# New durations in the planner of a two-block kernel, and a guard between two rotary tasks

## The chip, the cores and the metric

The kernel runs on one core of a Trainium2 chip. The metric is device microseconds for one launch; the kernel before was timed three times. Throughout, TensorE's columns of the trace are called PE (matmuls) and PEld (weight loads), VectorE is DVE, ScalarE is ACT, GpSimd is POOL, and SyncE, which issues all DMAs here, is SP.

## The reference

256 rows of width 2048, fp32, go through two blocks.

```python
x = x + attention(rms_norm(x, mixer_norm))            # 32 query heads, 4 key heads of 64, window 128
x = x + swiglu(rms_norm(x, ffn_norm))                 # 5632 wide
for l in range(2):                                    # second block
    mod = silu(c) @ ada_w[l] + ada_b[l]               # shift, scale, gate
    h = rmsnorm(x, g_pre[l]) * (1 + scale) + shift
    y = mlstm_mixer(h) if l == 0 else band_attention_mixer(h, k, v)
    x = x + gate * rmsnorm(y, g_post[l])
```

Queries and keys of the first block are normalised per head and rotated (rotary embedding, `apply_rope`). The mixer of l = 0 projects to 8 heads of q, k (256 wide) and v, o, z (512 wide), convolves q and k over time, forms a decay-weighted 256 x 256 product for each head, and multiplies the normalised result by sigmoid(o) * silu(z). For l = 1, keys and values come from a modulated copy of x, and 16 heads of 128 attend over a band with a bias.

## The kernel before, in words

**Weights.** Every weight matrix streams from memory once, in slots of 2 x 128 rows by 512 columns (`strm`, tile `w`). Each slot is split into a high part by ACT (`wh`, a cast to fp32r) and the rest by DVE (`wl`). With the activations split likewise (`xh`, `xl` or `ah`, `al`), one product is three fp32r matmuls. A k-tile of a chunk (128 rows, here called a step) is 12 matmuls of 256 columns or 6 of 512; a slot is two steps. There are 816 slots. These are the main matmuls (tile `mm`).

**Stages.** P1 is the attention block (`kv_task`, `att_task`, `att_half` beside the projections), P2 the FFN, P3 the mLSTM mixer (per head a chunk of q and k, then v, o, z; `conv_task`, `num_task`, `y_task`), P4 the band attention (`band_head`). From the start of P2 on, the modulation vectors are computed beside all this on DVE: 256 mv steps (`mv_run`), each with a load of 512 KB and two multiply-adds on `mvacc`; after 8 of them `mv_reduce` splits the sum (`acch` on ACT, `accl` on DVE) and lets PE sum over partitions with two pairs of matmuls (tile `bg`).

**The planner.** The program's order is fixed on the host while it is built. A `Clock` keeps one planned time for each engine. The wrapper `Eng` adds a planned duration for each instruction as it is emitted (lines 46 to 67); nothing of it runs on the chip. Everything beside the main matmuls is a Python generator in a queue `bgq`. After each step of main matmuls, `pump` asks `due` of each task:

```python
if task[2]:
    return task[1] + LAG <= clk.eng["pe"]
return (task[1] <= clk.eng["pe"] + task[4]
        and max(clk.eng["v"], clk.eng["s"]) <= clk.eng["pe"] + LOAD)
```

`task[1]` is the planned end of the task's last instruction, `LAG` is 0.3, `LEAD` (the usual `task[4]`) 1.0 and `LOAD` 6.0 planned us. The first branch is that of a part with matmuls: it goes into PE's order behind the first step that ends at least 0.3 planned us after its inputs. Each engine runs its own instructions in the order in which they were emitted, so a background matmul that stands too early makes PE wait. `stall` advances the tasks without main matmuls between, where the next chunk needs a result. The planner knows neither DMA times nor a wait for a buffer, nor table loads of ACT. A generator that yields `HOLD` is asked again at the next pump. `mv_step` starts an mv step when the planned time of the last one's next load, 5.0 planned us after it, is at most 0.3 ahead of PE's clock.

**norm_rope** (lines 589 to 609) takes a tile of heads through its mean of squares, the multiplication with the result, two POOL products into `rb`, a DVE product into `rc` and a DVE sum. `rb` and `rc` have one buffer each.

Of the kernel before, what the change touches and what calls it, by code (L numbers as in the profile page):

```python
# [11 lines left out]
F32R = mybir.dt.float32r  # L12
# [31 lines left out]


class Eng:
    RATE = {"v": 1.0 / 960, "s": 1.0 / 1400, "g": 1.0 / 480}
    BASE = {"v": 0.13, "s": 0.26, "g": 0.15}

    def __init__(self, eng, key, clock):  # L50
        self._e, self._k, self._c = eng, key, clock
# [1 line left out]
    def __getattr__(self, name):  # L53
        fn = getattr(self._e, name)

        def f(*a, **k):
            dst = k["out"] if "out" in k else a[0]
            n = int(np.prod(dst.shape[1:]))
            if self._k == "pe":
                m = k["rhs"] if "rhs" in k else a[2]  # L60
                fast = m.dtype == F32R
                dur = max(n, 256) / 2400 if fast else 4 * max(n, 64) / 2400
            else:
                dur = self.BASE[self._k] + n * self.RATE[self._k]
            self._c.spend(self._k, dur)
            return fn(*a, **k)  # L66
        return f
# [13 lines left out]
def kernel(ctx: ExitStack, tc: tile.TileContext, i: dict, out: bass.AP):  # L81
# [45 lines left out]
    sc = keep.tile([P, KD], F32, name="sc")  # L127
    ident = kc[:, K_ID:K_ID + P]

# [1 line left out]
    PF, SP = 4, 3  # L131
    order = []
    loaded = {}
# [29 lines left out]
    HOLD = 16  # L163
# [118 lines left out]
    plan = []  # L282
# [27 lines left out]
        for c in range(width, 4):  # L310
            add_chunk(chs[c])

# [1 line left out]
    mv = {"gen": None, "pace": 0.0, "acc": 0.0, "t": 0.0, "done": set(), "sent": set()}  # L314
    gt = {}

# [84 lines left out]
    busy = {"kv", "tab", "rst"}  # L401
# [21 lines left out]
        while lab not in mv["done"]:  # L423
            stall()

# [1 line left out]
    def rstd(dst, ss, n):  # L427
        shp = list(ss.shape)
        v = small.tile(shp, F32, tag="rv", bufs=2, name="rv")
        r = small.tile(shp, F32, tag="rr", bufs=2, name="rr")  # L430
        q = small.tile(shp, F32, tag="rq", bufs=2, name="rq")
        V.tensor_scalar(v, ss, 1.0 / n, EPS, op0=ALU.mult, op1=ALU.add)
        V.tensor_scalar(r.bitcast(I32), v.bitcast(I32), -0.5, 1597463007.0, op0=ALU.mult, op1=ALU.add)
        for it in range(3):
            V.tensor_mul(q, r, r)
            V.scalar_tensor_tensor(q, q, -0.5, v, op0=ALU.mult, op1=ALU.mult)
            V.scalar_tensor_tensor(dst if it == 2 else r, q, 1.5, r, op0=ALU.add, op1=ALU.mult)
# [82 lines left out]
        wrote("a", kt0, n, 2 if sl is None else 1)  # L520
        free(1)

# [1 line left out]
    p1 = ExitStack()  # L524
    q1 = p1.enter_context(tc.tile_pool(name="p1", bufs=1))
    make_identity(nc, ident)
# [62 lines left out]
    def norm_rope(src, H, w, t, dst):  # L589
        n = H * 64  # L590
        s3 = src.rearrange("p (h d) -> p h d", d=64)
        sq = q1.tile([P, CW], F32, tag="sq", bufs=1, name="sq")
        S.activation(sq[:, :n], src, ACTF.Square)
        ss = q1.tile([P, H], F32, tag="ss", bufs=2, name="ss")
        V.tensor_reduce(ss, sq[:, :n].rearrange("p (h d) -> p h d", d=64), AX.X, ALU.add)
        ri = q1.tile([P, H], F32, tag="ri", bufs=2, name="ri")
        rstd(ri, ss, 64)
        ri = ri.unsqueeze(2)
        yield
        V.tensor_mul(s3, s3, ri.to_broadcast([P, H, 64]))  # L600
        b = q1.tile([P, 8, 64], F32, tag="rb", bufs=1, name="rb")
        ta, tb = tab[:, w, t, 0], tab[:, w, t, 1]
        G.tensor_mul(b[:, :H, 0:32], s3[:, :, 32:64], tb[:, 0:32].unsqueeze(1).to_broadcast([P, H, 32]))
        G.tensor_mul(b[:, :H, 32:64], s3[:, :, 0:32], tb[:, 32:64].unsqueeze(1).to_broadcast([P, H, 32]))
        c = q1.tile([P, 8, 64], F32, tag="rc", bufs=1, name="rc")[:, :H]
        V.tensor_mul(c, s3, ta.unsqueeze(1).to_broadcast([P, H, 64]))
        yield
        V.tensor_add(dst, c, b[:, :H])
        yield

    def kv_task(kv):
        k3 = big[:, 0:1536].rearrange("p (a b c) -> p a b c", a=2, b=4)
        V.memset(k3, 0.0)
        while "tab" in busy:
            yield HOLD
        for t in range(2):
            yield from norm_rope(kv[:, t], 4, 1, t, k3[:, t, :, 64:128])
        for gg in range(2):
            yield 2
            bs = []  # L620
            for g in (2 * gg, 2 * gg + 1):
                b = bank([P, 2, T])
                for t in range(2):
                    PE.transpose(b[:, 0, t * P:(t + 1) * P], k3[:, t, g, 64:192], ident)
                    PE.transpose(b[:, 1, t * P:(t + 1) * P], k3[:, t, g, 0:128], ident)
                bs.append(b)
            yield
            for j in range(2):
                S.copy(kpad[:, 2 * gg + j], bs[j])
                free(1)  # L630
        busy.discard("kv")
# [5 lines left out]
    def att_task(g, qs):  # L637
        while "tab" in busy:
            yield HOLD
        for t in range(2):  # L640
            yield from norm_rope(qs[:, t], 8, 0, t, qs[:, t].rearrange("p (h d) -> p h d", d=64))
        qT = q1.tile([P, 2, 4, P], F32, tag="qT", bufs=2, name="qT")
        yield 2
        bs = []
        for t in range(2):
            b = bank([P, 4, P])
            for j in range(4):
                PE.transpose(b[:, j], qs[:, t, j * P:(j + 1) * P], ident)
            bs.append(b)
        yield  # L650
        for t in range(2):
            S.copy(qT[:, t], bs[t])
            free(1)
        add_bg(att_half(g, 0, qT))
        add_bg(att_half(g, 1, qT))
# [68 lines left out]
        yield  # L724
        hilo(4 * g, b, 4, slice(t * P, (t + 1) * P))

    # P1 plan
    def kv_done(ps):
        while "rst" in busy:
            stall()  # L730
        clk.cur = clk.eng["pe"]
        kv = q1.tile([P, 2, 256], F32, name="kv")
        for t in range(2):
            S.activation(kv[:, t], ps[t][:, 0:256], ACTF.Copy, scale=rst[:, t:t + 1])
            S.activation(vsb[:, t], ps[t][:, 256:512], ACTF.Copy, scale=rst[:, t:t + 1])
        add_bg(kv_task(kv))
# [47 lines left out]
    add_out([mk("tok", wload(i["w_o"], 0, n * CW), "a", KD, wo_done(n)) for n in range(4)], [4, 6], 3)  # L784
    will("x", 0, KD)

    # P2 plan
    pools = {}

    def enter2():  # L790
# [64 lines left out]
            chs[3].done, chs[3].part = None, down_part  # L855
        add_out(chs, [nk // SL - 2], 2)

    # P3 plan
    def ahead(gen, n):
        for _ in range(n):  # L860
            next(gen)
        add_bg(gen, 8.0)
# [224 lines left out]
                chs[3].done, chs[3].part = None, lambda ps, t: aout_half(ps, t, 3, 1)  # L1087
            add_out(chs, [6], 2)

    # P4 plan  # L1090
    qz = big[:, D:].rearrange("p (a k t) -> p a k t", a=2, t=T)
    def enter4():
        drain()
# [181 lines left out]
    chs[3].done, chs[3].part = None, fin_part  # L1275
    add_out(chs, [6], 2)

# [1 line left out]
    def start_stats():  # L1279
        for n in range(4):  # L1280
            yield
            for t in range(2):
                sumsq(q1, x[:, t, n * CW:(n + 1) * CW], ssx[:, t, n:n + 1])
        x_rstd()
        busy.discard("rst")
        yield
        S.activation(sc, cols[:, C_C:C_C + KD], ACTF.Silu)
# [88 lines left out]
```

## Time and profile before

| | us |
|---|---|
| runs, in order of time | 2548.68, 2553.22, 2559.36 |
| median | 2553.22 |
| the profiled execution, its span | 2553.0 (no other time of it is given) |
| PE busy in it | 2492.9 (98%) |
| DVE busy | 1783.5 (70%) |
| ACT busy | 1222.0 (48%) |
| POOL busy | 167.4 (7%) |
| mean DMA rate | 225 GB/s |
| mean granted TensorE clock | 0.990 |

Nearly all instructions have line 66 of the wrapper, so the trace is read by tiles and by stretches. PE is busy almost throughout; what matters is where it isn't, and what it waits for there. The page counts 34863 instructions.

### The profile page before, as it was taken

What the parts mean: (1) busy time and instruction counts of PE and PEld (TensorE: products, weight loads), DVE (VectorE), ACT (ScalarE), POOL (GpSimd) and SP (SyncE); (2) the same over time, 40 slices, a digit from 0 to 9 for tenths busy, and PEclk for the clock granted to TensorE, in tenths of its full rate; (3) what the DMA queues carried; (4) which work ended last, traced back from release to release, by engine and by line L of the source; (5) the groups of instructions that cost most, each with busy time, mean ns of one, the idle gap of its engine ahead of it and who ended that gap; (6) DMA issues with size and microseconds to landing.
All of it is one profiled execution on the core that took longest, in us unless ns stands there. A gap on an engine that the chain in (4) does not pass through costs nothing.

```text
span 2553.0 us, 34863 instructions
## 1 busy us (share of the span) xinstructions
PE 2492.9 (98%) x12816; PEld 2083.1 (82%) x12816; DVE 1783.5 (70%) x2788; ACT 1222.0 (48%) x1696; POOL 167.4 (7%) x174
## 2 busy tenths in 40 slices
PE   8999999999999999899999999999999989999998
PEld 6767888888888888778788778888888789899986
DVE  6885777777777777778778777765454564477755
ACT  5655544334443444555445444445444454455553
POOL 0231000000000000201101010001001120000000
PEclk9999999999999999999999999999999999999999
DMA  6434788888888887568878888856656546677854
GB/s 207 149 102 146 232 277 269 278 277 276 275 272 278 275 276 261 164 208 277 262 239 254 267 276 275 269 159 190 184 163 197 166 133 189 185 262 251 261 189 149
DMA packets 319083, 575.57 MB, mean 225 GB/s; under 512 B 21664, under 2 KB 56608, under 8 KB 318912
## 3 DMA queue, kind: packets, MB, share of 16 engines
q1 hardware_dynamic: 318912, 573.35, 69.7%
q8 instruction: 100, 1.64, 0.3%
q14 instruction: 71, 0.58, 0.1%
HBM read 571.18 MB, written 2.10 MB: 225 GB/s over the span
## 4 chain that ended last, share of the span: by engine, by line
PE 78%; issue 6%; DVE 6%; DMA 5%; ACT 3%; SPq 0%; POOL 0%; ACTq 0%; DVEq 0%; POOLq 0%
PE mm L66 73%; PE bg L66 5%; DMA w<-in_a_w_in_dram 4%; DVE wl L66 3%; ACT wh L66 2%; DVE mvacc L66 1%; DMA w<-in_b_w_in_dram 1%; DMA rb<-in_rel_dram 0%; DMA w<-in_a_w_out_dram 0%; DVE pr L66 0%; ACT sq L66 0%; DVE xl L66 0%; DMA x<-in_x_dram 0%; ACT big L66 0%; DVE big L66 0%
## 5 line engine op out<-in xcount | busy, mean ns | idle before, releaser
L66 DVE TENSOR_TENSOR wl<-w,wh 128x1024 fp32r<-128x1024 f32 x816 | 1010.3, 1243 | 627.9 <-ACT wh L66 616.9
L66 ACT CAST wh<-w 128x1024 fp32r<-128x1024 f32 x816 | 853.4, 1050 | 947.9 <-PE mm L66 747.6
L66 PE MATMUL mm<-wh,xh 128*128 128x512 f32 x1760 | 702.5, 399 | 0.0
L66 PE MATMUL mm<-wh,xl 128*128 128x512 f32 x1760 | 696.5, 396 | 4.1 <-DVE xl L66 4.1
L66 PE MATMUL mm<-wl,xh 128*128 128x512 f32 x1760 | 696.4, 396 | 1.7 <-DVE wl L66 1.7
L66 DVE SCALAR_TENSOR_TENSOR mvacc<-mvt,sc,mvacc 128x512 f32<-128x512 f32 x512 | 393.0, 768 | 11.6 <-DMA mvacc<-in_ada_b_dram 1.6
L66 PEld LDWEIGHTS mm<-wh,xl 128*128 128x128 f32 x1760 | 331.0, 188 | 85.2 <-DVE xl L66 5.0
L66 PEld LDWEIGHTS mm<-wl,xh 128*128 128x128 f32 x1760 | 331.3, 188 | 79.8 <-DVE wl L66 2.2
L66 PEld LDWEIGHTS mm<-wh,xh 128*128 128x128 f32 x1760 | 331.3, 188 | 79.1 <-issue 2.3
L66 PE MATMUL mm<-xh,wh 128*128 128x256 f32 x1280 | 367.8, 287 | 8.2 <-DVE xh L66 8.2
L66 PE MATMUL mm<-xl,wh 128*128 128x256 f32 x1280 | 364.5, 285 | 0.8 <-DVE xl L66 0.7
L66 PE MATMUL mm<-xh,wl 128*128 128x256 f32 x1280 | 362.8, 283 | 0.0
L66 PE MATMUL mm<-wh,al 128*128 128x512 f32 x864 | 341.9, 396 | 3.3 <-DVE al L66 3.3
L66 PE MATMUL mm<-wh,ah 128*128 128x512 f32 x864 | 345.0, 399 | 0.0
L66 PE MATMUL mm<-wl,ah 128*128 128x512 f32 x864 | 341.7, 395 | 0.1
L66 PEld LDWEIGHTS mm<-xh,wh 128*128 128x128 f32 x1280 | 246.6, 193 | 11.0 <-DVE xh L66 6.1
L66 PEld LDWEIGHTS mm<-xl,wh 128*128 128x128 f32 x1280 | 246.2, 192 | 3.5 <-DVE xl L66 3.0
L66 PEld LDWEIGHTS mm<-xh,wl 128*128 128x128 f32 x1280 | 245.9, 192 | 0.0
L66 PEld LDWEIGHTS mm<-wh,al 128*128 128x128 f32 x864 | 162.5, 188 | 43.0 <-DVE al L66 3.8
L66 PEld LDWEIGHTS mm<-wh,ah 128*128 128x128 f32 x864 | 162.4, 188 | 41.5 <-issue 4.0
L66 PEld LDWEIGHTS mm<-wl,ah 128*128 128x128 f32 x864 | 162.4, 188 | 38.5 <-issue 0.7
L66 POOL TENSOR_TENSOR so<-so,sz 128x512 f32<-128x512 f32 x16 | 30.4, 1897 | 713.5 <-ACT sz L66 370.3
(187 smaller groups left out, 1405.2 us busy)
## 6 DMA issues: line engine op xcount, KB each, us to landing
mvt<-in_ada_dram SPq DMA_DIRECT2D x192, 512.0 KB
w<-in_a_w_in_dram SPq DMA_DIRECT2D x192, 512.0 KB
w<-in_w_gate_dram SPq DMA_DIRECT2D x88, 512.0 KB
w<-in_w_up_dram SPq DMA_DIRECT2D x88, 512.0 KB
w<-in_w_down_dram SPq DMA_DIRECT2D x88, 512.0 KB
mvt<-in_kv_ada_dram SPq DMA_DIRECT2D x64, 512.0 KB
w<-in_a_w_in_dram SPq DMA_DIRECT2D x128, 256.0 KB
w<-in_a_w_out_dram SPq DMA_DIRECT2D x64, 512.0 KB
```

The costliest lines, as they stand in the source:

```text
L66: return fn(*a, **k)
```

## The change

The table of planned durations is replaced: rates and bases for DVE, ACT and POOL, an extra for instructions with an accumulator output, the input's size for a reduction, a rate of its own for a POOL memset, and for PE a figure per column for fp32r, a fixed 0.109 us for a transpose, and half the fp32 cost where one side has 64 rows or columns. In `norm_rope` a task waits while another holds the word "rope", from before the multiplication to after the sum. The other edits are comment lines.

```diff
-    RATE = {"v": 1.0 / 960, "s": 1.0 / 1400, "g": 1.0 / 480}
-    BASE = {"v": 0.13, "s": 0.26, "g": 0.15}
+    RATE = {"v": 1.0 / 960, "s": 1.0 / 1200, "g": 1.0 / 300}
+    BASE = {"v": 0.15, "s": 0.18, "g": 0.15}
+    ACCUM = {"v": 0.08, "s": 0.19, "g": 0.0}
...
-                fast = m.dtype == F32R
-                dur = max(n, 256) / 2400 if fast else 4 * max(n, 64) / 2400
+                if name == "transpose":
+                    dur = 0.109
+                elif m.dtype == F32R:
+                    dur = max(n, 240) * 0.4557e-3
+                else:
+                    dur = max(4 * n / 2400, 0.215)
+                    if a[1].shape[0] == 64 or a[1].shape[1] == 64:
+                        dur /= 2
             else:
-                dur = self.BASE[self._k] + n * self.RATE[self._k]
+                if name in ("tensor_reduce", "memset"):
+                    n = int(np.prod((dst if name == "memset" else a[1]).shape[1:]))
+                rate = 1.0 / 1200 if self._k == "g" and name == "memset" else self.RATE[self._k]
+                dur = self.BASE[self._k] + n * rate
+                if k.get("accum_out") is not None:
+                    dur += self.ACCUM[self._k]
...
         rstd(ri, ss, 64)
         ri = ri.unsqueeze(2)
         yield
+        while "rope" in busy:
+            yield HOLD
+        busy.add("rope")
         V.tensor_mul(s3, s3, ri.to_broadcast([P, H, 64]))
...
         V.tensor_add(dst, c, b[:, :H])
+        busy.discard("rope")
         yield
```

## Rows read from the trace of the kernel before

**Rows 1.** Windows: stretch, its length, busy time and count by engine, clock, DMA.

```profile
0.00:33.00 33.00, 21.73 (x95) 16.89 (x95) 17.68 (x57) 22.13 (x45) 0.71 (x6) 1.00 0.68 224
33.00:233.00 200.00, 194.85 (x858) 145.38 (x858) 155.29 (x424) 116.21 (x255) 52.11 (x54) 0.98 0.44 137
233.00:980.00 747.00, 747.00 (x3296) 604.04 (x3296) 560.48 (x753) 320.84 (x367) 7.80 (x15) 1.00 0.82 268
980.00:1090.00 110.00, 102.25 (x536) 86.12 (x535) 83.48 (x142) 52.82 (x81) 13.66 (x16) 0.95 0.62 199
1090.00:1672.00 582.00, 570.34 (x2911) 476.71 (x2910) 443.80 (x635) 279.69 (x355) 43.22 (x30) 0.99 0.79 257
...
2016.00:2070.00 54.00, 42.05 (x215) 36.47 (x214) 39.55 (x88) 27.10 (x51) 13.67 (x16) 0.84 0.33 99
...
2240.00:2440.00 200.00, 198.42 (x1654) 195.83 (x1653) 155.99 (x296) 110.65 (x183) 3.55 (x18) 1.00 0.79 258
2440.00:2553.00 113.00, 102.78 (x495) 84.93 (x494) 60.73 (x86) 47.08 (x65) 3.63 (x3) 0.97 0.49 162
```

**Rows 2.** Waits of PE's matmuls: whose, for whom, total us, times, longest.

```profile
PE bg L66 <- POOL y L66: 6.0, 5, 2.1
...
PE mm L66 <- DVE al L66: 3.3, 1, 3.3
...
PE bg L66 <- DVE accl L66: 2.6, 4, 0.7
```

**Rows 3.** The chain of waits in order of time: start, us, what.

```profile
195.03 1.75 PE bg L66 x16
...
340.87 37.79 PE mm L66 x162
...
2292.25 2.83 PE mm L66 x24
```

**Rows 4.** Groups of instructions, shapes apart: busy us, mean ns; idle before.

```profile
L66 DVE TENSOR_TENSOR wl<-w,wh 128x1024 fp32r<-128x1024 f32 x816 | 1010.3, 1243 | 627.9 <-ACT wh L66 616.9 <-PE bg L66 0.5
L66 ACT CAST wh<-w 128x1024 fp32r<-128x1024 f32 x816 | 853.4, 1050 | 947.9 <-PE mm L66 747.6 <-DMA w<-in_a_w_in_dram 101.7 <-DMA w<-in_b_w_in_dram 29.4
...
L66 POOL TENSOR_TENSOR so<-so,sz 128x512 f32<-128x512 f32 x16 | 30.4, 1897 | 713.5 <-ACT sz L66 370.3 <-DVE mvacc L66 343.2
...
L66 POOL TENSOR_TENSOR rb<-qs,tab 128x256 f32<-128x256 f32 x16 | 18.8, 1196 | 51.3 <-DVE qs L66 51.3
...
L66 ACT ACTIVATE big<-big,nm 128x256 f32<-128x256 f32 x32 | 15.8, 501 | 0.0
```

**Rows 5.** Timeline in P3, a head's end: start, us, engine, operation, [idle before].

```profile
1257.82 1.53 DVE L66 SCALAR_TENSOR_TENSOR mvacc<-mvt,sc,mvacc 128x512 f32<-128x512 f32 x2
...
1260.57 0.28 PE L66 MATMUL mm<-xh,wh 128*128 128x256 f32 x1
...
1262.87 1.81 POOL L66 TENSOR_TENSOR so<-so,sz 128x512 f32<-128x512 f32 x1 [79.43 <-DVE mvacc L66]
...
1267.92 3.45 DVE L66 SCALAR_TENSOR_TENSOR mvacc<-mvt,sc,mvacc 128x512 f32<-128x512 f32 x2
...
1269.05 0.27 PE L66 MATMUL bg<-kc,y 128*128 128x128 f32 x1
1269.24 1.59 POOL L66 TENSOR_TENSOR y<-y,so 128x512 f32<-128x512 f32 x1
...
1270.88 0.98 PE L66 MATMUL bg<-kc,y 128*128 128x128 f32 x7 [1.56 <-POOL y L66]
...
1272.43 0.41 DVE L66 TENSOR_TENSOR accl<-mvacc,acch 128x256 fp32r<-128x256 f32 x1
...
1272.90 0.58 PE L66 MATMUL bg<-accl,onesr 128*128 128x256 f32 x1 [0.65 <-DVE accl L66]
```

**Rows 6.** Timeline, the middle of a head in P3.

```profile
1228.80 0.42 DVE L66 TENSOR_TENSOR accl<-mvacc,acch 128x256 fp32r<-128x256 f32 x1
...
1229.45 0.28 PE L66 MATMUL bg<-accl,onesr 128*128 128x256 f32 x1
```

## The prediction

> **What bounds the kernel now.** I read the windows first. PE is busy for 2492.9 of 2553.0 us, so 60.1 us are idle, and length minus busy time of each stretch says where [rows 1]: 11.3 in the first 33 us, 5.1 in the rest of P1, none in P2 (233 to 980), 7.8 at the change to P3 (980 to 1090), 11.7 in the part of P3 that carries mv steps (1090 to 1672), none in the rest of P3, 12.0 at the change to P4 (2016 to 2070), 1.6 among the band heads (2240 to 2440), 10.2 at the end; half a us is left for the stretch not shown. Only the order of instructions can change, so no busy time goes away. Nor can all of the idle time. The first 33 us are loading and the first tiles, the end is one serial chain behind the last matmuls, and the two changes of stage are serial chains (sum, root, rows, modulation) that the code writes out straight behind a `drain`. What a better order can reach is 5.1 + 11.7 + 1.6 = 18.4 us, 0.7% of the span. Then the waits: in P3 most is PE waiting for POOL's `y`, 6.0 in five pieces, and for DVE's `accl`, 2.6 in four; in P1 once 3.3 for `al` [rows 2].
>
> **The change, part by part.** *PE's clock.* In P2 a main matmul of 512 columns starts every 37.79 / 162 = 0.233 us, one of 256 columns in P4 every 2.83 / 24 = 0.118 [rows 3]. The old plan has 512 / 2400 = 0.213 and 0.107, the new one 512 x 0.0004557 = 0.233 and 0.117. A step thus takes 1.28 planned us before and 1.40 after, and 1.40 to 1.42 in truth. Sixteen transposes took 1.75 us, 0.109 each [rows 3]; the old plan has 0.213. A chunk with its 16 transposes was planned about right in sum and wrong in its parts; now both are right. What it removes is a hidden margin: by the old plan the real PE came to a placed matmul 0.12 us later per step than planned. For a part that is placed four steps behind its start, that is 0.5 us.
>
> *ACT and DVE.* The split of a slot: `wh` 0.99 planned before, 1.03 after, 1.050 in the trace; `wl` 1.20, 1.22, 1.243 [rows 4]. An exponential of 256 columns with its sum goes from 0.44 to 0.58; the trace has 0.501 for the instruction without the reading of the sum [rows 4]. So the planned attention gets longer, by 16 x 0.14 or 2.2 us for two halves at most. Its parts are asked for later: safer for PE inside, later at the end of P1, where w_o already waits 3.3 for `al` [rows 2]. Bounds: the 5.1 idle us of P1 go, or the 2.2 come on top. I take nothing, between them.
>
> *POOL, the largest correction.* A product of 512 columns was planned at 0.15 + 512 / 480 = 1.22 and is now 0.15 + 512 / 300 = 1.86; the trace has 1.897 [rows 4]. At each head's end `y_task` runs four in a row, then the transposes of `y` follow. Old plan: 1.25 (two ACT passes) + 4.87 + 0.3 = 6.4 behind the end of the head, that is 5.02 steps, so behind the sixth. In the trace the next head starts at 1260.57 and the transposes at 1269.05, 8.5 us or six steps later; POOL ends at about 1270.83, and PE waits 1.56 [rows 5]. New: 1.21 + 7.43 + 0.3 = 8.94, or 6.4 steps, so behind the seventh, one step or 1.4 us later. Of the 1.56 some 0.15 stays. The pattern stands four times, where mv steps run; 6.0 us in all [rows 2], of which 1.4 at each can go: 5.1 gained, counting that two of the waits are shorter than a step.
>
> But the next thing is late too. Right behind the transposes come two matmuls of `mv_reduce`; `accl` ends at 1272.43 + 0.41 = 1272.84, and PE waits again, 0.65 [rows 5]. With the transposes a step later, these two stand ahead of them in PE's order, if the planner finds them due behind the sixth step. PE would come to them at about 1269.1 and wait until 1272.84, 3.7 us in place of 1.56 + 0.65 = 2.2, with the transposes no longer filling 1 us of it. So bounds at each of the four places are a gain of 1.4 and a loss of 1.5. I take half of the gain: 2.6 of the 5.1.
>
> Why `accl` is late: two mv multiply-adds took 3.45 us beside POOL's products and 1.53 without them [rows 5]; the planner charges 1.33 before and 1.37 after, whatever POOL does. [...]
>
> *The memset of POOL and the order of mv steps.* A memset is planned shorter, and a reduction by its input; both are off PE's path, covered by POOL's and DVE's idle time [rows 1]. The spacing of mv steps hardly moves. One may follow another after 5.0 - 0.3 = 4.7 planned us: three steps are 3.84 before and 4.20 after, four are 5.12 and 5.60, so four in both, unless background matmuls fall between. The loads behind it on SP's queue keep their order then, and the 268 GB/s of P2 stay [rows 1]. If three became usual, the share of 0.82 of the DMA engines would be the cover to go; I price that with the slower rival.
>
> *Margins elsewhere.* In the middle of a head `accl` ends at 1229.22 and its matmul starts at 1229.45, 0.23 us later [rows 6]; three others, at 1330, 1432 and 1622, have 0.22 to 0.24. With 0.5 us of margin gone at four such places, 4 x (0.5 - 0.23) is a loss of 1.1. Bounds: nothing, or a whole step earlier, 4 x 1.2 = 4.8 lost; or a gain of the same if the longer planned DVE chain puts them a step later, which has nothing to win as PE does not wait there. I take 1.1. In P4 a better price of the exponentials may remove a part of the 1.6; I take 1.0, between 1.6 and a loss of the same.
>
> *The guard.* It adds a wait on the host only, in `bgq`. Held back is the next group's first multiplication, with two products on POOL of 1.196 [rows 4] and the DVE sum behind it, and whoever waits for that group: at the end w_o. Where groups do not meet it costs nothing; where they do, one section, 2 x 1.2 on POOL and about the same on DVE, 5 us at most, and only if it hits the last groups. If it keeps an older group ahead of a younger one, part of the 3.3 for `al` can go. I take 0.
>
> Sum: 2553.0 - 2.6 + 1.1 - 1.0 = 2550.5 for the span. The median of the runs stands 0.2 above that span, so 2550.7; I say 2551.
>
> **The rivals.** *The wait changes its name.* PE stops waiting for `y` and waits for `accl` instead, since DVE's 3.45 stays: the 2.6 gained in P3 are 0, the time 2553. For it: 1272.84 comes after POOL's end at 1270.83. Against: mv steps may fall elsewhere in a head.
>
> *Nothing moves.* Places are quantised by steps of 1.4 us, and P2 has no idle time to win; the time is 2553 too. For it: two matmuls due at the same step keep their order. Against: by the arithmetic above the transposes of `y` cross a step.
>
> *The waits nearly all go.* Everything in P3's mv part (11.7), P4's 1.6 and half of P1's 5.1 goes: 2553.0 - 15.9 = 2537. For it: with true durations of PE, transposes and POOL each background matmul lands behind its inputs. Against: table loads, DMA waits and POOL's effect on DVE stay unplanned, and 0.65 of each pair is DVE's own lateness.
>
> *Margins eaten (slower).* The place is the pairs of `mv_reduce` and their like in P3's mv part and in P4, 16 jobs of two pairs. If half of the 32 come a step earlier against slacks like the 0.23 of [rows 6], each costs 1.4 - 0.23 = 1.2: 19 us, 2572. It decides from the point where the planned chain falls short of the real one by more than LAG and slack, 0.3 + 0.23. For it: DVE's queue waits for late slots (idle before `wh` from DMA, 102 us in all [rows 4]), unplanned. Against: DVE's planned durations rise by 2% while PE's rise by 9%, but chains on DVE and ACT with accumulators rise more.
>
> **How the numbers follow.** Under 0.5% of 2553, 12.8 us, a measurement of this kernel can hardly be told from no change; the bounds are 2540 and 2566. The forecast has a chance of 0.36, with a range of its own of 2542 to 2559; the wait that changes its name 0.10; nothing moved 0.08; the waits gone 0.25; margins eaten 0.21. Of the case of waits gone 0.03 stay inside the bound, and so do 0.03 of the slower one; the forecast spills 0.03 to either side. That makes faster 0.25, same 0.54, slower 0.21. The range leaves out a third of the fast case and half of the slow one: 2533 to 2570.
>
> **What would show it.** Right: the transposes of `y` start seven steps (9.9 us) behind a head's first matmul and the 6.0 for `y` fall below 2; the idle time of 1090 to 1672 is 8 to 11; mv loads still come every second slot. Wrong: `accl` takes over more than 6 us of waits (the first rival), the idle time of 33 to 233 passes 10 (the guard or the attention's order), P2 gets idle time, or the stretches at 980 and 2016 change by more than 3 us, which I hold to be fixed.

## The result, and the profile after

The changed kernel takes 2575.25 us (median of 4 runs, 2571.97 to 2576.17) against 2553.39 before: a ratio of 1.0076, 95% interval 1.0059 to 1.0093. The forecast was 2551, the range ended at 2570: wrong in sign and in size. The profiled execution has a span of 2574.4 us, 21.4 more than before.

The windows after, at the same places of the program (their bounds moved by what the kernel had lost by then), answer to [rows 1]; the columns are the same.

```profile
0.00:33.00 33.00, 23.90 (x99) 18.89 (x100) 18.92 (x59) 22.53 (x46) 0.71 (x6) 0.99 0.67 224
33.00:238.00 205.00, 195.71 (x850) 144.85 (x849) 153.44 (x422) 114.41 (x251) 51.48 (x51) 0.97 0.43 133
238.00:997.00 759.00, 756.19 (x3307) 604.49 (x3306) 561.60 (x758) 322.06 (x372) 10.56 (x19) 1.00 0.81 265
997.00:1107.00 110.00, 100.81 (x530) 84.69 (x529) 82.55 (x137) 51.89 (x80) 14.35 (x15) 0.95 0.63 198
1107.00:1695.50 588.50, 572.61 (x2908) 479.23 (x2907) 445.64 (x636) 279.80 (x355) 43.56 (x30) 0.99 0.78 254
...
2039.50:2093.70 54.20, 41.44 (x218) 34.94 (x217) 39.73 (x88) 27.18 (x51) 14.51 (x16) 0.91 0.32 98
...
2263.70:2461.00 197.30, 196.94 (x1649) 195.45 (x1648) 156.36 (x297) 109.46 (x182) 3.57 (x18) 1.00 0.81 263
2461.00:2574.40 113.40, 102.87 (x500) 85.04 (x498) 59.05 (x84) 46.88 (x64) 3.63 (x3) 0.97 0.48 159
```

Length minus PE's busy time gives idle times of 9.3 us in P1 behind 33 us (5.1 before), 2.8 in P2 (none before), 15.9 in P3's mv part (11.7), 0.4 among the band heads (1.6). But PE's idle time grew by only 10.6 us in all (60.1 to 70.7), and its busy time, for the same 12,816 matmuls, by 10.8 (2492.9 to 2503.7). So half of the loss is not in the idle column at all. P2's window is 12 us longer with only 2.8 us idle.

What shows it is an alignment. Both kernels run the same 11,712 main matmuls in the same order, so the start of the k-th in one trace less its start in the other is the time lost up to there. The table gives how much this grows over a stretch, in us, for the changed kernel and for every kernel told of below (bounds by the index of the main matmul; the first stretch moves by 2 us and more between kernels whose order there is the same, so it is left out of the reasoning; the expectations below still count it with P1):

```
                     start    P1     P2   change  P3, mv  middle  band   end    sum
matmul index         0-300  -720   -3960  -4350   -6950   -9750  -11250
changed kernel        -1.9   +6.9  +12.1   -0.2    +6.6   +0.1   -4.3   +1.8  +21.1
PE alone              +2.5   -3.7  +12.4   +1.0   +10.6   -1.0   +6.9   -0.6  +28.1
POOL alone            -0.4  +12.4   +0.0   +0.0    -5.6   +0.1   -1.8   +0.0   +4.7
DVE and ACT alone     -3.4   +9.5   +0.1   +0.2    -4.7   +1.8   -5.3   +2.1   +0.2
PE undone             -4.8  +10.5   -0.0   -0.2   -14.3   +0.6   -5.0   +2.1  -11.1
pair later            -2.9   +6.8   +3.4   +0.2    -7.3   +0.1   -3.6   +2.3   -0.9
split from PE's time  -3.1   +8.0   +0.6   +0.6    +9.4   +0.1   -3.9   +1.8  +13.4
P1 early, pair 2.8    -1.6   +3.0   +5.7   +0.2   -11.0   +0.9   -1.1   +0.0   -4.0
before, pair later    +1.4   +0.2   -0.1   -0.1    -8.8   +0.2   -2.3   +0.2   -9.3
y on DVE              -2.1   +7.8  +11.6   -0.7    -5.0   +0.1   -3.5   +1.8   +9.9
before, pair, y DVE   -2.1   +1.3   -0.1   -0.2   -11.2   +0.2   -1.3   +0.2  -13.1
the same, P4 new      +1.0   +0.2   -0.1   +1.1   -13.8   +0.4   -1.8   +1.4  -11.6
P1 old, pair later    +2.0   +0.2   +3.5   +0.7   -10.9   +0.1   -3.6   +2.3   -5.7
P1 old, LAG 1.7       +1.0   +0.2   +0.2   -1.7   -15.2   +0.1   -6.2   +2.8  -18.8
P1 and PE old         +0.6   +0.2   +0.0   +0.5   -12.2   +1.2   -3.4   +2.1  -11.1
the same, y on DVE    +0.9   +0.2   +0.1   -0.2   -14.5   +0.6   -5.9   +2.1  -16.7
```

Each row is one execution. For most rows its time lies within 2.5 us of the kernel's median; "POOL alone" lies 7.1 under it, "y on DVE" 5.6 under, "P1 and PE old" 4.8 over. "before, pair, y DVE" and "the same, P4 new" have one order of PE up to the band heads, and still differ by 2.6 us in P3's mv part, 1.3 at the change to P3 and 1.1 in P1; P2 agrees to 0.1. A smaller difference than that shows nothing by itself.

The changed kernel loses in P1, P2 and P3's mv part, and wins among the band heads. PE's waits that answer to [rows 2]:

```profile
PE bg L78 <- ACT acch L78: 12.3, 5, 4.0
...
PE bg L78 <- DVE pr L78: 7.7, 2, 7.4
...
PE bg L78 <- DVE accl L78: 1.2, 1, 1.2
...
PE mm L78 <- DVE al L78: 0.6, 1, 0.6
```

The waits for `y` are gone, and waits for `acch` have come: 12.3 us for 6.0.

**P2.** The timeline of one job's end (a job is the 8 mv steps of one sum), after the change:

```profile
517.60 1.05 ACT L78 CAST wh<-w 128x1024 fp32r<-128x1024 f32 x1 [1.74 <-PE mm L78]
...
518.68 1.23 DVE L78 TENSOR_TENSOR wl<-w,wh 128x1024 fp32r<-128x1024 f32 x1 [0.59 <-ACT wh L78]
...
519.82 1.53 DVE L78 SCALAR_TENSOR_TENSOR mvacc<-mvt,sc,mvacc 128x512 f32<-128x512 f32 x2
...
521.36 0.40 PE L78 MATMUL mm<-wh,al 128*128 128x512 f32 x1
...
521.38 0.41 ACT L78 CAST acch<-mvacc 128x256 fp32r<-128x256 f32 x1 [2.74 <-DVE mvacc L78]
...
521.82 0.42 DVE L78 TENSOR_TENSOR accl<-mvacc,acch 128x256 fp32r<-128x256 f32 x1 [0.47 <-ACT acch L78]
...
521.84 0.39 PE L78 MATMUL bg<-acch,onesr 128*128 128x256 f32 x1
...
522.30 0.39 PE L78 MATMUL bg<-accl,onesr 128*128 128x256 f32 x1
...
522.53 0.40 PE L78 MATMUL mm<-wh,ah 128*128 128x512 f32 x1
```

and the same job in the kernel before:

```profile
516.10 0.42 DVE L66 TENSOR_TENSOR accl<-mvacc,acch 128x256 fp32r<-128x256 f32 x1
...
518.28 0.28 PE L66 MATMUL bg<-acch,onesr 128*128 128x256 f32 x1
...
518.40 0.28 PE L66 MATMUL bg<-accl,onesr 128*128 128x256 f32 x1
...
518.52 0.39 PE L66 MATMUL mm<-wh,ah 128*128 128x512 f32 x1
```

Before, `accl` ended at 516.52 and its matmul started 1.88 us later; at the 15 jobs of P2 this slack is 1.88 to 2.65. After, the pair stands three steps earlier in PE's order (behind main matmul 1830 in place of 1848), right behind `acch`, and waits for both parts of the sum: from 521.36 to 522.53 there are 1.17 us, of which one main matmul and the pair need 0.233 + 0.117 + 0.117 = 0.47. That is 0.70 lost, at 14 of the 15 jobs: 9.8 of the 12.1. Another 1.2 is the wait for `accl` in the list above, at the last pair of the stretch, ahead of main matmul 3960. The row of the pair's first matmul has no idle time in brackets, because the profile still counts the matmul in front of it as busy for 0.40 us, for a pitch of 0.233.

**P3.** The end of P3's first head, after ([rows 5] show the next head of the kernel before):

```profile
1183.59 2.66 DVE L78 SCALAR_TENSOR_TENSOR mvacc<-mvt,sc,mvacc 128x512 f32<-128x512 f32 x2
...
1186.17 4.55 DVE L78 TENSOR_TENSOR wl<-w,wh 128x1024 fp32r<-128x1024 f32 x2
...
1187.37 2.27 POOL L78 TENSOR_TENSOR so<-so,sz 128x512 f32<-128x512 f32 x1
...
1190.65 2.53 DVE L78 SCALAR_TENSOR_TENSOR mvacc<-mvt,sc,mvacc 128x512 f32<-128x512 f32 x2
...
1193.67 0.58 PE L78 MATMUL bg<-acch,onesr 128*128 128x256 f32 x1 [4.02 <-ACT acch L78]
...
1197.07 1.91 PE L78 MATMUL bg<-kc,y 128*128 128x128 f32 x8
```

The transposes of `y` stand one step later and wait for nothing, but the pair is now ahead of them. DVE, which takes 4.55 us for two differences of 1.23 beside POOL's products, gives `acch` its sum at 1193.2, and PE stands for 4.02 us. Behind the wait PE runs at about half pace: a main matmul starts every 0.21 us, and every 0.118 from 1199.83 on. Windows of the wait and of the 5 us behind it:

```profile
1189.70:1193.60 3.90, 0.00 (x0) 0.00 (x0) 3.44 (x3) 0.39 (x2) 2.59 (x2) 0.92 0.86 259
1194.40:1199.40 5.00, 5.00 (x24) 5.00 (x25) 3.82 (x8) 2.38 (x5) 0.53 (x1) 0.50 0.76 218
```

The granted clock of those 5 us is 0.50, the lower of the two levels seen there (1.00 and 0.50), and PE had stood still from 1189.65 on before it fell, at about 1193.0. The eight transposes take 1.91 us; seven took 0.98 in [rows 5]. Five us at half pace are, as an estimate from these rows, 2.5 us that this wait costs beyond its own length. Nearly the whole loss of P3 stands at this one head: 6.7 us between main matmuls 4560 and 4740. At the ends of the next four heads, where PE waited for `y` before, waits for `acch` have taken their place, and the four together come to -0.7 us.

**P1.** PE and DVE where w_o begins:

```profile
156.82 0.68 DVE L78 TENSOR_REDUCE ss<-sq 128x8 f32<-128x512 f32 x1
...
160.77 0.68 DVE L78 TENSOR_TENSOR qs<-qs,ri 128x512 f32<-128x512 f32 x1
...
162.10 0.68 DVE L78 TENSOR_TENSOR rs<-rs,es 128x8 f32<-128x8 f32 x1
...
163.06 1.19 DVE L78 TENSOR_SCALAR pr<-pr,rs 128x128 f32<-128x128 f32 x4
...
163.66 0.72 PE L78 MATMUL bg<-kc,pr 128*128 128x128 f32 x2 [7.43 <-DVE pr L78]
```

w_o's first steps need attention rows that are not there yet, so the planner places all the attention that is outstanding in one run behind main matmul 504: 21.0 us, 7.4 of them a wait for `pr`. DVE reaches `pr` only at 163.06, behind the norm of another group (from 156.82 on) that stands ahead of it in its queue. Before, the run at that place was 6.9 us long, and 3.3 us of waiting for `al` followed [rows 2]. Here too the wait costs more than it lasts: from 163.7 to 168.0 the granted clock is 0.50.

### The profile page after: what moved, and what is told of

Its sections match the earlier page's. It is cut to its first block, busy times and chain, and to the rows that moved or that the text cites. A ratio compares the mean times of both kernels' runs of the same rounds, so it can differ in the third digit from the quotient of the medians.

```text
span 2574.4 us, 34916 instructions
## 1 busy us (share of the span) xinstructions
PE 2503.7 (97%) x12816; PEld 2084.1 (81%) x12816; DVE 1784.0 (69%) x2788; ACT 1220.2 (47%) x1696; POOL 171.3 (7%) x174
## 4 chain that ended last, share of the span: by engine, by line
PE 71%; DVE 9%; issue 8%; DMA 6%; ACT 4%; POOL 0%; SPq 0%; ACTq 0%; DVEq 0%; POOLq 0%
PE mm L78 66%; PE bg L78 5%; DVE wl L78 3%; DMA w<-in_a_w_in_dram 3%; ACT wh L78 3%; DVE mvacc L78 3%; DMA w<-in_b_w_in_dram 1%; DMA w<-in_w_up_dram 0%; DVE xl L78 0%; DVE accl L78 0%; ACT acch L78 0%; DVE pr L78 0%; DVE big L78 0%; ACT sq L78 0%; DVE rq L78 0%
## 5 line engine op out<-in xcount | busy, mean ns | idle before, releaser
L78 ACT CAST wh<-w 128x1024 fp32r<-128x1024 f32 x816 | 853.0, 1049 | 918.8 <-PE mm L78 705.7
L78 DVE SCALAR_TENSOR_TENSOR mvacc<-mvt,sc,mvacc 128x512 f32<-128x512 f32 x512 | 393.2, 768 | 11.2 <-DMA mvacc<-in_ada_b_dram 1.6
L78 PEld LDWEIGHTS mm<-xh,wh 128*128 128x128 f32 x1280 | 244.7, 191 | 11.7 <-DVE xh L78 6.6
```

## The experiments

Times are medians; ratios are against the kernel before on the same chip, with 95% intervals.

**PE's durations alone**, on the kernel before.

```diff
-                fast = m.dtype == F32R
-                dur = max(n, 256) / 2400 if fast else 4 * max(n, 64) / 2400
+                if name == "transpose":
+                    dur = 0.109
+                elif m.dtype == F32R:
+                    dur = max(n, 240) * 0.4557e-3
...
```

> The kernel before with the new planned durations of PE alone (matmuls and transposes). Aligned by the index of the main matmul, the changed kernel loses 5.0 us on the one before in P1, 10.4 in P2 (0.7 at each of its 15 jobs of mv), 1.5 at the change to P3, 6.6 in P3's mv part, and wins 2.4 in P4. Theory A (the true PE clock makes the planner find the mv_reduce pair due two main steps behind the job's last mv step instead of four, and the real DVE is later than planned): P2 loses 9 to 11 here too, the total is 2560 to 2572. Theory B (the longer ACT and DVE durations or POOL's move the pair): P2 stays within 1 us of the kernel before, the total 2548 to 2558.

2584.40 us, 1.0116 (1.0099 to 1.0133). P2 loses 12.4, or 11.0 without the pair ahead of main matmul 3960, which the expectation counts with the change of stage: Theory A, at the upper end of its range. P3 loses 10.6 and the band heads 6.9 as well, so the total is above what either theory allowed. PE's new durations alone account for P2's loss, and are slower than the entire change. Which of PE's prices does it (fp32r columns, transposes, plain fp32) was not taken apart.

**POOL's durations alone**, on the kernel before (`"g": 1.0 / 300`, and 1/1200 for its memset).

> The kernel before with POOL's new rate and its memset price alone. Theory A: P2 stays within 1 us of the kernel before; in P3 the transposes of y come a step later and the waits for y (6.0) fall below 2, but the mv_reduce pairs then stand ahead of them and wait for acch, so P3's mv part stays within 4 us either way; P1 moves by up to 3. Total 2549 to 2560. Theory B: P2 loses 5 or more.

2566.51 us, 1.0042 (1.0026 to 1.0058). P2 is unmoved (0.0), P3 gains 5.6: no wait for `y` is left, and `acch` and `accl` take 8.1. P1 loses 12.4, far outside the 3 expected. Theory A stands for P2; P3's gain is above its 4, P1 was misjudged, and the total is above its range. The execution in the table is the fastest of seven: the median lies 9.8 us above that of the kernel before, where the table sums to 4.7, and no trace shows the rest.

**DVE's and ACT's durations alone**, on the kernel before.

```diff
-    RATE = {"v": 1.0 / 960, "s": 1.0 / 1400, "g": 1.0 / 480}
-    BASE = {"v": 0.13, "s": 0.26, "g": 0.15}
+    RATE = {"v": 1.0 / 960, "s": 1.0 / 1200, "g": 1.0 / 480}
+    BASE = {"v": 0.15, "s": 0.18, "g": 0.15}
+    ACCUM = {"v": 0.08, "s": 0.19, "g": 0.0}
...
+                if k.get("accum_out") is not None:
+                    dur += self.ACCUM[self._k]
```

> The kernel before with the new durations of DVE and ACT alone (rates, fixed parts, the price of a sum read out, the reductions by their input). Theory A: P2 stays within 1 us of the kernel before; P1 loses 3 to 7, since w_o begins with more of the attention outstanding; total 2553 to 2563. Theory B: P2 loses 5 or more.

2555.49 us, 0.9997 (0.9986 to 1.0008). P2 +0.1; P1 +9.5 (6.1 with the first stretch, as the expectation counts it, which is inside its 3 to 7); P3 -4.7 and the band heads -5.3 pay it back. Theory B is out: of the three groups of durations only PE's moves P2.

The guard alone, on the kernel before, gives the same instructions in the same order on every engine, so it has no run. Nor have the changed durations without the guard.

**The pair one step later**, on the changed kernel.

```diff
             V.tensor_sub(hl[1], acc[:, fs], hl[0].bitcast(F32))
+            clk.cur += 1.4
             yield 1
```

> The changed kernel, with 1.4 planned us (one main step) added behind the split of an mv sum, ahead of its two matmuls. Theory A: every pair comes one main step later; P2 gets back 9 to 10.4 us of the 10.4, P3's mv part 2 to 5 of its 6.6; total 2558 to 2565. Rival (the loss of P2 is not from the early pair but from what the pair's PSUM bank and the later instructions block): P2 gets back under 3, total 2570 or more.

2553.45 us, 0.9992 (0.9983 to 1.0002): all of the loss but nothing more, and under the range expected. P2 gets back 8.7 of 12.1, by the expectation's 9 to 10.4 a little too few; P3 gets back 13.9, about three times what was expected. Waits for `acch` fall from 12.3 to 0.8, and the slow clock behind them goes too: the changed kernel has a granted clock of 0.50 to 0.51 over 17 us of P3's mv part (1193.0 to 1199.8, 1394.4 to 1397.8, 1496.8 to 1500.2, 1687.9 to 1691.3), this one over 3 (from 1185.0); the mean over the whole span is 0.989 there and 0.992 here. What P2 still loses stands where the pair meets the transposes of `sg`: the first of them takes 0.39 us to the next in place of 0.11; in the changed kernel the pair, and its wait, stood a step ahead of them.

**The split charged from PE's time**, on the changed kernel. DVE's difference and ACT's cast of a weight slot can start when PE has released the buffer (the casts of the changed kernel stand 705.7 us in all for PE's main matmuls); the planner charges them as soon as their engine is free.

```diff
             w = loaded.pop(j)
-            clk.cur = 0.0
+            clk.cur = clk.eng["pe"]
```

> The changed kernel; the planner charges the split of a weight slot (the cast on ACT, the difference on DVE) from the planned time of PE, at which the slot's buffer comes free, not from the moment its engine is free. In P2 of the changed kernel the plan ends a job's last multiply-add 0.8 us behind the start of the next main step, the trace 2.55 us behind it. Theory A1 (this lateness is the split, which waits for its buffer): with the split charged so, the pairs of P2 fall four steps behind the last mv step, as in the kernel before, and P2 gets back 8 to 11 of the 12; P3's pairs keep their steps in the plan, so P3 stays within 3 us of the changed kernel; total 2561 to 2568. Rival A2 (the lateness is something else on DVE's queue, and grows with the plan): P2 gets back under 4, total 2570 or more.

2566.49 us, 1.0049 (1.0034 to 1.0064). P2 gets back 11.5 of 12.1; P3 loses 9.4, within 3 us of the changed kernel's 6.6. A1 holds for P2; the pairs stand one step ahead of where the kernel before has them. There, DVE is later than planned because its queue stands at a split that waits for its buffer; the rows of P2 above show it (`wh` waits for PE until 517.60, `wl` for `wh` until 518.68, the multiply-adds stand behind it). In P3 this is not enough.

**Background in P1 early, the pair 2.8 us later**, on the kernel with the later pair (`LAG` -0.5 in P1, 0.3 behind it).

> The kernel with the pair one step later, changed twice, in two stretches that can be told apart by the index of the main matmul: the pair comes 2.8 planned us behind its split instead of 1.4, and in P1 alone background matmuls are due 0.5 planned us ahead of their inputs instead of 0.3 behind. Theory A: P2, which still loses 3.4 us on the kernel before where the pair meets the transposes of sg, loses under 1; P1, where w_o begins with attention outstanding and PE stands for it, loses 4.0 now and comes between a gain of 4 and a loss of 2; total 2541 to 2551. Rival: what P2 still loses comes from the longer plan in other ways, and PE in P1 only waits at other instructions: both within 1.5 us of the kernel with the pair one step later, total 2550 to 2556.

2551.44 us, 0.9986 (0.9974 to 0.9998); the interval overlaps that of the kernel with the later pair (0.9983 to 1.0002). P1 loses 3.0 in place of 6.8 (1.4 in place of 4.0 as the expectation counts, inside its range). P2 loses more, 5.7, where under 1 was expected: the transposes of `sg` now stand ahead of the pair and wait 3.3 us in ten places. So other background matmuls than the pair had come early too, and one edit for the pair uncovers the next.

**The pair later, old durations**, on the kernel before.

> The kernel before (old durations), with the same 1.4 planned us behind the split of an mv sum. It tells whether the gain of P3's mv part (7.3 us on the kernel before, with the new durations and the later pair) needs the new durations. Theory A (the waits of P3 come from pairs and transposes of y placed by luck of the step, and the new POOL rate puts the transposes right): P3's mv part gains 1 to 4 of the 7.3, since the waits for y (6.0) stay; P2 and P1 within 1 us; total 2550 to 2555. Rival (the later pair alone does it): P3 gains 6 or more, total 2544 to 2549.

2543.80 us, 0.9962 (0.9948 to 0.9977). P3 gains 8.8, so the rival holds: the later pair alone does it. The waits for `y` stay (5.4). The kernel before had waits of this kind as well.

**The products of y on DVE, PE's order unchanged**, on the changed kernel.

```diff
+    VG = Eng(nc.vector, "g", clk)
...
-            G.tensor_mul(so[:, t], so[:, t], sz[:, t])
-            G.tensor_mul(y[:, t], y[:, t], so[:, t])
+            VG.tensor_mul(so[:, t], so[:, t], sz[:, t])
+            VG.tensor_mul(y[:, t], y[:, t], so[:, t])
```

> The changed kernel with the four products of y_task issued on DVE instead of POOL, and charged by the planner as on POOL, so that PE's order is the same to the last instruction. In the changed kernel PE waits 12.3 us for acch, in five places of P3, while DVE takes 2.27 us for a difference of 1.23 and 2.53 for a pair of multiply-adds of 1.53 beside POOL's products. Theory C (DVE and POOL hold each other up): DVE does the four products in about 2.8 us and its other instructions at their usual length; the waits for acch fall to 9 or less, total 2566 to 2573. Rival D (the place of the pair alone decides; DVE's queue is as long either way): waits for acch stay at 11 to 14, total 2573 to 2578.

2570.25 us, 1.0068 (1.0052 to 1.0085). The same head's end on DVE:

```profile
1187.93 0.69 DVE L78 TENSOR_TENSOR y<-y,so 128x512 f32<-128x512 f32 x1
1188.54 1.22 DVE L78 TENSOR_TENSOR wl<-w,wh 128x1024 fp32r<-128x1024 f32 x1
1189.68 1.53 DVE L78 SCALAR_TENSOR_TENSOR mvacc<-mvt,sc,mvacc 128x512 f32<-128x512 f32 x2
```

A product takes 0.69 us where POOL took 1.3 to 2.3, the difference 1.22 in place of 2.27, the multiply-adds 1.53 in place of 2.53. Although DVE does four more instructions, its sum is ready earlier, and the waits for `acch` fall to 6.7: Theory C holds in this, that DVE is slower beside POOL's products, by 1.05 us for the difference and 1.00 for a pair of multiply-adds. In the trace P3 gets back 11.6, which is more than the 5.6 by which the waits are shorter; a clock of 0.50 occurs nowhere in its mv part here, and the mean over the span is 0.992, against 0.989 for the changed kernel. But this execution is the fastest of four; by the ratios to the kernel before, 1.0068 against 1.0076 for the changed kernel, it wins 2 us, and the intervals overlap, so the gain in time is not shown clear of noise.

**The pair later and the products of y on DVE**, on the kernel before.

> The kernel before (old durations) with the pair of an mv sum 1.4 planned us later and the four products of y_task issued on DVE, charged by the planner as on POOL (PE's order is that of the kernel with the later pair). Theory C (the products on POOL are slow themselves and hold DVE up): the waits for y, 5.4 us in four places, fall below 1.5, P3's mv part gains 12 to 15 us on the kernel before where the later pair alone gains 8.8; total 2537 to 2542. Rival D (DVE's queue, lengthened by the four products, makes another input late): P3 gains under 9, total 2543 or more.

2539.21 us, 0.9951 (0.9937 to 0.9965). The waits for `y` are gone; P3 gains 11.2, a little under the 12 to 15 expected. The 2.4 more than with the later pair alone are within what two executions of one order differ by (the next kernel has 13.8 there), and the intervals of the two overlap.

**The same, with DVE's and ACT's new durations in P4.**

> As the kernel with the later pair and the products of y on DVE, and from the start of P4 on the planner takes the new durations of DVE and ACT, with old ones for PE and POOL. With the new DVE and ACT durations alone the band heads gained 5.3 us on the kernel before, with the later pair alone 2.3. Theory A (each stretch has its own margin, the gain is that of the exponentials' sums in P4): 2 to 4 us less in P4 than without it, total 2534 to 2540. Rival (P4's gain comes from how P3 ends): the same time within 1 us in P4.

2541.33 us, 0.9955 (0.9940 to 0.9971). The band heads gain 1.8 against 1.3: Theory A fails, the 5.3 that these durations gained alone don't come from P4's own prices. The rival's number came, but that the gain comes from how P3 ends was not tested.

**Old durations in P1, the pair later.**

```diff
+            if self._c.p1:
...
+                    dur = (dict(v=0.13, s=0.26, g=0.15)[self._k]
+                           + n / dict(v=960, s=1400, g=480)[self._k])
...
     def enter2():
+        clk.p1 = False
```

> The changed kernel with the pair one main step later (1.4 planned us) and the old durations up to the end of P1, the new ones behind it. Theory E (P1's loss is the new durations of POOL, DVE and ACT, by which attention is placed later and w_o begins with more of it outstanding): P1 loses under 1 us on the kernel before instead of 4.0, the other stretches stay as in the kernel with the later pair; total 2547 to 2552. Rival F (the guard, or the lengths in themselves): P1 loses 3 or more.

2547.13 us, 0.9976 (0.9963 to 0.9990). P1 loses 0.2 in place of 6.8: Theory E holds. (With the first stretch, as the expectation counts, it is 2.2 in place of 4.0.) On every engine the order is that of the kernel before up to the end of P1, with the guard in the kernel. So the new durations make P1's loss, and the guard by itself does not; what it does beside the new durations is not shown.

**PE's durations undone**, on the changed kernel.

> The changed kernel with the old planned durations of PE; POOL, DVE, ACT and the guard as changed. Theory A: the pairs of P2 fall four steps and more behind a job's last mv step again, P2 loses under 1 us on the kernel before instead of 12, P3's mv part gains 3 to 8; P1 loses 4 to 12, as with the new POOL or the new DVE and ACT durations alone; total 2550 to 2562. Theory B (the longer durations together move P2's pair): P2 loses 5 or more, total 2565 or more.

2543.36 us, 0.9962 (0.9949 to 0.9976), below the range expected. P2 0.0; P3 gains 14.3, twice what was thought; P1 loses 10.5. Without PE's part the change would have been a gain of 0.4%. The waits that are left in P3:

```profile
PE bg L72 <- POOL y L72: 0.9, 1, 0.9
...
PE bg L72 <- DVE accl L72: 0.7, 2, 0.4
```

**True durations with a larger margin.** Old durations in P1, all new ones behind it, no edit of the pair.

```diff
-    LAG, LEAD, LOAD = 0.3, 1.0, 6.0
+    LEAD, LOAD = 1.0, 6.0
+    lag = [0.3]
...
     def enter2():
+        clk.p1 = False
+        lag[0] = 1.7
```

> The changed kernel with the old durations up to the end of P1, and all the new ones, PE's too, behind it; from P2 on a background matmul is due 1.7 planned us behind its inputs instead of 0.3 (the condition on mv steps keeps its 0.3). If what the true PE durations took away is only distance between the plan and a DVE that is later than planned (margin), then one larger margin for all background matmuls gives it back: P1 within 1 us of the kernel before, P2 loses under 4 instead of 12, P3's mv part gains 5 to 12; total 2540 to 2549. Rival (true PE durations hurt in another way, by the step at which mv steps and their loads come): P2 still loses 6 or more, total 2552 or more.

2536.65 us, 0.9927 (0.9913 to 0.9942). P1 +0.2, P2 +0.2, P3's mv part -15.2, band heads -6.2. No wait for `y`, `acch` or `accl` stands in the list of PE's waits any more (two pairs of P3, ahead of main matmuls 4488 and 5424, still take 0.7 us more than their columns need), and its windows in P2 and P3's mv part are:

```profile
235.00:982.00 747.00, 747.00 (x3297) 604.42 (x3294) 563.89 (x760) 321.14 (x368) 7.90 (x15) 1.00 0.82 270
...
1091.00:1657.50 566.50, 564.42 (x2922) 472.74 (x2920) 439.29 (x632) 278.75 (x354) 41.14 (x30) 1.00 0.80 262
```

P2 has the length of before, and 2.1 us are idle in P3's mv part where there were 11.7 before and 15.9 after the change. From P2 on it is not the true durations that cost time, but the margin that went with the false ones. P3's gain and the total are better than expected. The old durations with the same larger margin have no run, and neither has a larger margin in P1; so how much of this gain needs the new durations is open.

**The change without PE's part, old durations in P1.**

> The change without its PE durations, and without any new duration in P1: old PE durations throughout, the new ones of POOL, DVE and ACT from P2 on, the guard. If the stretches add up: P1 0 (within 1), P2 0, P3's mv part -14, P4 -5 to -3; total 2534 to 2539, below every kernel so far. Rival (the gain of P3 with the old PE durations came from the later state in which P1 left the planned clocks): P3 gains under 9, total 2541 or more.

2538.94 us, 0.9933 (0.9919 to 0.9946): P3 -12.2, the stretches add up to within 2 us. Its interval overlaps that of the kernel with the larger margin (0.9913 to 0.9942).

**The same, y on DVE.**

> The same with the four products of y_task on DVE, charged as on POOL. If the waits for y and acch are gone already in the kernel without this edit: within 2 us of it. If POOL's products still make DVE late there: 2 to 5 us less.

2537.43 us, 0.9930 (0.9917 to 0.9942), within 2 us of the kernel without it, which has waits of 1.8 us for `y` and 1.5 for `accl` in all. Between these two, POOL beside DVE costs nothing that the runs show: 2538.94 against 2537.43, and the intervals overlap.

## Why the prediction was wrong

- **What bounds the kernel.** The step that failed first: "Only the order of instructions can change, so no busy time goes away", and from it "What a better order can reach is 18.4 us". PE's busy time moved by 10.8 us for the same matmuls, half of the loss. The 18.4 came out near (the best kernel gains 18.8 in the trace) by luck: P3 gave 15.2 for the 11.7 that were read, the band heads 6.2 for 1.6, P1 nothing for 5.1. P2 was left out because it had no idle time; it lost 12.1. The numbers to read there were the slack of its pairs, 1.88 to 2.65 us, and how far the new plan moves them, three steps of 1.4.
- **PE's clock.** This is the term that was mis-sized. That the false clock held a hidden margin was in the text ("0.12 us later per step", 0.5 us for four steps); but at 14 of the 15 jobs of P2 the pair moved by three whole steps, 4.2 us. "Margins elsewhere" has 1.1 lost at four places of P3 and nothing for P2; PE's durations alone lost 12.4 in P2, 10.6 in P3 and 6.9 in the band heads. Why the plan moves three steps is only argued: where PE is planned slower, DVE's planned work has more time between two steps, so a sum's planned end comes nearer to PE's clock, by more than the sum of four steps' 0.12. The slower rival had the right mechanism, pairs that come early, with a chance of 0.21. That its 2572 lies near the measured 2575 is luck: it put 19 us in P3 and P4, and the loss was 12.1 in P2 and 6.6 in P3 while the band heads gained 4.3.
- **POOL.** Right: the transposes of `y` come one step later and the 6.0 us are gone; with POOL's durations alone P3's mv part gains 5.6, twice the 2.6 taken. Wrong: what follows beside PE's new durations. `acch` then takes 12.3, as the first rival has it ("the wait changes its name"); at one head that loses 6.7, where the worst bound was 1.5 at each place. The bound took DVE's lateness from one row and left out the clock: behind the 4.0 us wait, 5 us ran at 0.50, and the kernel before had such stretches too (0.51 from 1272.6 to 1276.0, behind the waits of [rows 5]). The parts don't add: PE's +10.6, POOL's -5.6 and DVE's and ACT's -4.7 come to 0.3, and the change has +6.6.
- **DVE and ACT in P1.** "I take nothing": measured +6.9 between matmuls 300 and 720, outside both bounds. The loss is not longer planned attention as such. Attention is placed later, and one long run at w_o's start exposes DVE's serial chain. For POOL's new durations P1 had no term; alone they cost 12.4 there.
- **The guard: 0.** Alone it changes no instruction's place.
- **The order of mv steps.** Right: the trace has two weight loads between any two mv loads in P2, before and after. P2's DMA rate went from 268 to 265 as P2 became longer.
- **The changes of stage** moved by 0.2 us and less, as forecast. **P4** gained 4.3 where 1.0 was taken.
- **The signs.** Of the signs of being wrong that it named, two came: P2 got idle time (2.8 us), and more than 6 us are spent waiting for the mv sum, for `acch` where it names `accl`.

What stays open: why the pairs of P2 move by just three steps; why the band heads gain 5 us with the new DVE and ACT durations in every stage and nothing with them in P4 alone; which of the two, POOL's or DVE's and ACT's durations, decides P1, where each alone costs more than all together; and whether the old durations with a larger margin would have done as well.

## What to carry to other kernels

A planner's wrong numbers can hold its margin: before correcting a duration, measure the slack between each placed instruction and its last input, compare the new plan's places with the old ones, and give back as an explicit margin what the correction takes away (1.7 us in place of 0.3, with P1 left as it was, made this change a gain of 0.7%). A stretch without idle time can still lose, as P2 did here (12.1 us), and of a wait not all need show as idle time (at the pair of P2 shown above 0.16 of the 0.70 us lost, between 520.90 and 522.60): align two traces by the index of an instruction that both run in the same order. A wait that replaces another should be priced with what comes behind it on the queue, the clock included (0.50 for 5 us behind the wait of 4.02 us).

## What the runs showed of the hardware

A wait of PE cost more than it lasted: at P3's first head the changed kernel lost 6.7 us with a wait of 4.02. Behind that wait the granted clock was 0.50 for 5 us, the lower of the two levels seen there (1.00 and 0.50); behind those of 2.35 (ended at 1394.46), 2.39 (1495.24) and 2.17 us (1686.81) the mean over the next 4 to 5 us was 0.74, 0.59 and 0.62, part of it at either level; behind one of 1.33 (1294.80) it was 1.00. The rows, each the stretch behind one of the last four waits, in order of time:

```profile
1295.50:1300.00 4.50, 4.50 (x39) 4.47 (x39) 4.24 (x9) 2.93 (x6) 0.53 (x1) 1.00 0.74 231
...
1395.30:1400.00 4.70, 4.70 (x32) 4.70 (x32) 4.12 (x9) 2.38 (x5) 0.52 (x1) 0.74 0.75 227
...
1496.00:1500.00 4.00, 4.00 (x18) 3.45 (x18) 3.70 (x8) 2.24 (x5) 0.52 (x1) 0.59 0.84 270
...
1687.50:1692.00 4.50, 4.50 (x27) 4.50 (x27) 3.60 (x5) 2.48 (x5) 0.00 (x0) 0.62 0.39 113
```
